# A two-layer decoder trunk in split fp32: the 512-column and the 256-column products of an output chunk, in two runs or turn about

## Chip, cores and metric

The kernel runs on one core of a Trainium2 chip, in one launch. The metric is the time of an execution on the device in microseconds (us); with one core, that core is the slowest. A profiled execution gives a span (first to last instruction) and a trace of every instruction.

## The reference, cut to what matters

A decoder trunk of two layers on 256 tokens of width 2048, all in fp32. Nearly all the work is products of a 256-row activation with a large weight matrix:

```python
def sq_relu_mlp(h, w1, w2):
    return jnp.square(jax.nn.relu(h @ w1)) @ w2          # w1 2048x8192, w2 8192x2048
...
    for l in range(DEPTH):                               # DEPTH = 2
        hn = rms_norm(x, mix_norm_g[l])
        x = x + (even_mixer(hn, ...) if l % 2 == 0 else odd_mixer(hn, ...))
        x = x + cross_attention(rms_norm(x, xattn_norm_g[l]), mem_n, xq_w[l], xk_w[l], xv_w[l], xo_w[l])
        x = x + sq_relu_mlp(rms_norm(x, mlp_norm_g[l]), mlp_w1[l], mlp_w2[l])
    return rms_norm(x, final_norm_g)
```

The even mixer is a convolution of 31 taps beside a differential attention, the odd mixer a gated convolution of 3 taps.

## The kernel before

**Split operands.** TensorE multiplies fp32r operands, which hold fewer bits than fp32, so each operand is split into a high part (the value rounded) and a low part (what is left). Weights come from memory as `raw` tiles (128x1024 f32, half of an output chunk's weights). ScalarE (ACT) casts `whi` from `raw`, and VectorE (DVE) subtracts to give `wlo`. An `Act` holds an activation with the high and the low part of each of its 16 blocks side by side, 256 columns each: `act.both(k)` is both (512 columns), `act.hi(k)` the high part alone (256 columns).

**An output chunk** is 128 output columns. It accumulates 16 blocks of 128 rows in one PSUM bank, and each block takes two products: high weights by both parts (512 columns wide), and low weights by the high part (256 columns). Two functions write them out:

- `long_run` (lines 217 to 225) has the whole chunk's four tiles `h[0], h[1], l[0], l[1]`. It issues fifteen 512-column products, then sixteen 256-column ones, then the last 512-column one, which closes the bank.
- `wide_piece` (lines 193 to 202) does the same with half a chunk, eight blocks: eight 512-column products (seven if this half closes the bank), eight 256-column ones, and the closing one.

By the code's loops 305 chunks go through `long_run` (the MLPs, most of the mixers' output projections and of the odd mixer) and 95 through `wide_piece` (the even mixer's projections, the keys of layer 0, the queries, and the first few chunks after a normalisation). That is 400 chunks, with 16 products of each width.

**What makes the tiles.** `weights` (line 178) loads, casts and subtracts for `wide_piece` and the mixers. In the MLPs an order written by hand does it: a `Chunk` (line 897) has `hi(g)` on ACT and `lo(g)` on DVE, or, where DVE is short of time, `lo_added(g)` (line 916): ACT writes the negated, rounded `raw` into `wlo`, and a DMA issued by GpSimd (POOL) adds `raw` to it in place (line 923). There are three `whi` and four `wlo` buffers, so tiles are made about one chunk ahead of their use.

**The MLP's order.** Its hidden layer comes in four quarters (`qd`). In each quarter 16 chunks of `w1` are followed by the `w2` part: eight times a `Step` (21 products of a fast 2x2 block scheme, tiles `sw`, `tw`, `b`, `hs`, PSUM tiles `p`), each followed by an output chunk of `w2` through `long_run`. The first of these, `outs[0]`, gets both its low halves by `lo_added`, first half 1 and then half 0 (lines 1213 and 1214), while the last chunk of `w1` runs:

```python
                if c == NC - 1 and seven:
                    n.lo_added(1)
                    n.lo_added(0)
```

This happens in each of four quarters of two MLPs, eight times in all.

**The even mixer's taps.** The 31 taps of eight channel blocks run on DVE (`cv`), dealt out a few per call of `weights` and put in one order with the `wlo` subtractions (the token "lo", line 190). They last until about 322 us, through the keys of layer 0.

TensorE (PE) issues in the order of the program. Outside the hand-ordered parts a scheduler places ACT's and DVE's instructions; it does so anew when the order on PE changes.

Of the kernel before, what the change touches and what calls it, by code (L numbers as in the profile page):

```python
# [45 lines left out]
def trunk(ctx: ExitStack, tc: tile.TileContext, d):  # L46
# [98 lines left out]
    def ordered(i, token):  # L145

        tc.stamp_issue_order_token(i.ins, token)
# [20 lines left out]
    def mm(*a, **k):  # L168
        i = T.matmul(*a, **k)  # L169
        if strict[0]:  # L170
            ordered(i, "pe")
# [21 lines left out]
    def wide_piece(ps, hi, lo, act, k, first, last):  # L193


        w = [slice(j * P, (j + 1) * P) for j in range(8)]
        for j in range(7 if last else 8):
            mm(ps, hi[:, w[j]], act.both(k + j), start=first and j == 0, stop=False)
        for j in range(8):
            mm(ps[:, :S], lo[:, w[j]], act.hi(k + j), start=False, stop=False)  # L200
        if last:
            mm(ps, hi[:, w[7]], act.both(k + 7), start=False, stop=True)

    def proj_group(srcs, act, order=(0, 1)):


        pp = [ps_mm.tile([P, 512], F32, tag="mm", name="mm") for _ in srcs]
        for g in order:
            if g == order[-1] and len(srcs) > 1:
                run_stages(END)  # L210
            for src, ps in zip(srcs, pp):
                hi, lo = weights(src[:, g * 1024:(g + 1) * 1024])
                first, last = g == order[0], g == order[-1]
                wide_piece(ps, hi, lo, act, g * 8, first, last)
        return pp

    def long_run(ps, h, l, act):

        w = [slice(j * P, (j + 1) * P) for j in range(8)]
        for k in range(15):  # L220
            mm(ps, h[k // 8][:, w[k % 8]], act.both(k), start=k == 0, stop=False)
        for k in range(16):
            mm(ps[:, :S], l[k // 8][:, w[k % 8]], act.hi(k), start=False, stop=False)
        mm(ps, h[1][:, w[7]], act.both(15), start=False, stop=True)
        return ps

    def proj_long(src, act):
        ps = ps_mm.tile([P, 512], F32, tag="mm", name="mm")
        h, l = zip(*[weights(src[:, g * 1024:(g + 1) * 1024]) for g in range(2)])
        return long_run(ps, h, l, act)  # L230
# [666 lines left out]
    class Chunk:  # L897
# [27 lines left out]
        def run(self, act, pool, tag):  # L925
            self.ps = long_run(pool.tile([P, 512], F32, tag=tag, name="mm"), self.h, self.l, act)
# [513 lines left out]
```

## Time and profile before

| | us |
|---|---|
| median of 3 runs | 2852.05 (2851.72 to 2854.14) |
| profiled execution | 2851.39 |
| its span | 2849.3 |
| PE busy | 2834.7 (99%) |
| PE weight loads busy | 2476.8 (87%) |
| DVE busy | 2318.8 (81%) |
| ACT busy | 1687.4 (59%) |
| POOL busy | 78.6 (3%) |

The profiled execution is 0.66 us under the median, and 2.1 us of it lie outside the span. An engine is busy while an instruction is open on it. Matmuls overlap their successors, so the distance from one start to the next, not the duration, is what a product costs. In rows of the timeline the columns are: start, time to the last end, engine, line, operation, what is written and read, sizes and count. Line 169 is the helper that issues every product, line 59 the one for ACT and DVE, so the rows are told apart by their tiles.

### The profile page before, as it was taken

The page shows a single profiled execution, that of the slowest core. Times are in us where ns is not written, and L with a number is a line of the kernel's source. Part 1 is how long each engine was busy: PE and PEld are TensorE (multiplying, and loading weights), DVE is VectorE, ACT ScalarE, POOL GpSimd, SP SyncE. Part 2 cuts the span into 40 slices and gives each one's busy share as a digit, 9 for nine tenths or more (in the row PEclk, how much of TensorE's full clock was granted, in tenths as well). Part 3 has the DMA queues.
Part 4 walks back from the last instruction along what each step waited for, and adds up shares of the span by engine and source line. Part 5 has one row for each costly group of instructions (what it writes and reads, how often), then busy time and mean ns, then how long its engine had stood idle before and what let it go on. Part 6 is the DMA issues. An engine that isn't in the chain of part 4 may idle for free.

```text
span 2849.3 us, 42240 instructions
## 1 busy us (share of the span) xinstructions
PE 2834.7 (99%) x15827; PEld 2476.8 (87%) x15827; DVE 2318.8 (81%) x3609; ACT 1687.4 (59%) x2365; POOL 78.6 (3%) x107
## 2 busy tenths in 40 slices
PE   9999999999999999999999999999999999999998
PEld 7888888898888888888888888888988888888887
DVE  7899987776788888888987787888777888888888
ACT  6666445555565665656654455676555656656566
POOL 0000000000000000000000000000000000000000
PEclk9999999999999999999999999999999999999999
DMA  7455665545686786967766666984455867769686
GB/s 247 162 183 176 191 193 187 172 151 177 194 255 197 223 241 200 265 193 236 214 201 199 197 208 222 255 259 151 149 177 192 258 207 220 233 201 265 193 243 170
DMA packets 213516, 588.23 MB, mean 206 GB/s; under 512 B 18240, under 2 KB 84160, under 8 KB 213312
## 3 DMA queue, kind: packets, MB, share of 16 engines
q1 hardware_dynamic: 200064, 538.48, 58.2%
q0 software_dynamic: 12672, 46.14, 8.2%
q8 instruction: 124, 2.03, 0.3%
q10 hardware_dynamic: 576, 0.92, 0.1%
q14 instruction: 80, 0.66, 0.1%
HBM read 537.23 MB, written 2.10 MB: 189 GB/s over the span
## 4 chain that ended last, share of the span: by engine, by line
PE 95%; DVE 2%; DMA 1%; ACT 1%; issue 0%; SPq 0%; DVEq 0%; ACTq 0%; POOLq 0%; POOL 0%
PE mm L169 75%; PE p L169 13%; PE mmr L169 4%; PE pox L169 1%; PE sx L169 1%; DVE wlo L59 1%; ACT whi L59 0%; DVE cv L59 0%; DMA wlo<-raw 0%; DVE x L59 0%; DMA raw<-w 0%; DMA raw<-even_in 0%; DMA raw<-odd_in 0%; DMA x<-xT 0%; PE nmr L169 0%
## 5 line engine op out<-in xcount | busy, mean ns | idle before, releaser
L59 ACT CAST whi<-raw 128x1024 fp32r<-128x1024 f32 (+1 forms) x849 | 890.3, 1050 | 398.5 <-PE mm L169 299.1
L59 DVE TENSOR_TENSOR wlo<-raw,whi 128x1024 fp32r<-128x1024 f32 (+1 forms) x761 | 924.1, 1220 | 94.3 <-ACT whi L59 84.2
L169 PE MATMUL mm<-xn,whi 128*128 128x512 f32 x3840 | 938.8, 392 | 0.0
L169 PEld LDWEIGHTS mm<-xn,whi 128*128 128x128 f32 x3840 | 701.7, 188 | 133.4 <-DVE xn L59 0.6
L169 PEld LDWEIGHTS mm<-xn,wlo 128*128 128x128 f32 x3840 | 501.0, 191 | 24.1 <-DVE wlo L59 0.2
L169 PE MATMUL mm<-xn,wlo 128*128 128x256 f32 x3840 | 509.0, 283 | 0.0
L59 ACT COPY sum<-mm 128x256 f32<-128x256 f32 x272 | 100.6, 371 | 382.9 <-PE mm L169 382.3
L169 PE MATMUL mm<-hid,whi 128*128 128x512 f32 x1024 | 253.3, 389 | 0.0
L59 ACT CAST tw<-raws 128x1024 fp32r<-128x1024 f32 x160 | 160.6, 1047 | 145.3 <-DVE raws L59 142.9
L59 DVE TENSOR_TENSOR raws<-raws 128x512 f32<-128x512 f32 x320 | 220.8, 690 | 7.7
L169 PEld LDWEIGHTS mm<-hid,whi 128*128 128x128 f32 x1024 | 192.5, 188 | 37.4
L59 DVE TENSOR_TENSOR sum<-mm,sum 128x256 f32<-128x256 f32 x240 | 101.0, 421 | 147.1 <-ACT sum L59 146.8
L59 DVE TENSOR_TENSOR tw<-raws,tw 128x1024 fp32r<-128x1024 f32 x160 | 189.6, 1222 | 26.5 <-ACT tw L59 24.9
L169 PE MATMUL p<-tw,hs 128*128 128x512 f32 x720 | 189.2, 389 | 0.0
L59 DVE TENSOR_TENSOR x<-x,mm 128x256 f32<-128x256 f32 x256 | 107.4, 420 | 80.9 <-PE mm L169 76.3
L169 PEld LDWEIGHTS p<-tw,hs 128*128 128x128 f32 x720 | 135.2, 188 | 28.0
L923 POOL DMA_DIRECT2D wlo<-raw x88 | 74.9, 855 | 2551.1 <-ACT wlo L59 1773.7
L169 PEld LDWEIGHTS mm<-hid,wlo 128*128 128x128 f32 x1024 | 131.1, 191 | 5.5 <-DMA wlo<-raw 0.7
L169 PE MATMUL mm<-hid,wlo 128*128 128x256 f32 x1024 | 132.9, 283 | 0.1
L169 PE MATMUL mm<-mem,whi 128*128 128x512 f32 x512 | 128.5, 392 | 0.0
L169 PE MATMUL mm<-o,whi 128*128 128x512 f32 x512 | 124.7, 392 | 0.0
L59 DVE TENSOR_TENSOR slo<-raws,shi 128x1024 fp32r<-128x1024 f32 x71 | 86.9, 1223 | 37.7 <-ACT shi L59 37.7
(224 smaller groups left out, 3235.4 us busy)
## 6 DMA issues: line engine op xcount, KB each, us to landing
raw<-w SPq DMA_DIRECT2D x384, 512.0 KB, 4.9
raws<-w SPq DMA_DIRECT2D x128, 512.0 KB, 5.3
raw<-odd_in SPq DMA_DIRECT2D x96, 512.0 KB, 4.8
wlo<-raw POOLq DMA_DIRECT2D x88, 512.0 KB, 7.4
raw<-even_in SPq DMA_DIRECT2D x64, 512.0 KB, 4.3
raw<-xk SPq DMA_DIRECT2D x64, 512.0 KB, 4.4
raw<-xq SPq DMA_DIRECT2D x64, 512.0 KB, 4.0
raw<-xo SPq DMA_DIRECT2D x64, 512.0 KB, 3.7
```

The source lines that it names most:

```text
L59: i = getattr(self.engine, name)(*a, **k)
L169: i = T.matmul(*a, **k)
L923: G.dma_start(out=self.l[g], in_=self.raw[g], accum_op=ALU.add)
```

## The change

In `wide_piece` and `long_run` the two runs become one loop over the blocks: the 512-column product of a block, then its 256-column product. The closing 512-column product of the bank stays last. The products, their operands and their number are the same.

```diff
@@ wide_piece
-        for j in range(7 if last else 8):
-            mm(ps, hi[:, w[j]], act.both(k + j), start=first and j == 0, stop=False)
         for j in range(8):
+            if not last or j < 7:
+                mm(ps, hi[:, w[j]], act.both(k + j), start=first and j == 0, stop=False)
             mm(ps[:, :S], lo[:, w[j]], act.hi(k + j), start=False, stop=False)
@@ long_run
-        for k in range(15):
-            mm(ps, h[k // 8][:, w[k % 8]], act.both(k), start=k == 0, stop=False)
         for k in range(16):
+            if k < 15:
+                mm(ps, h[k // 8][:, w[k % 8]], act.both(k), start=k == 0, stop=False)
             mm(ps[:, :S], l[k // 8][:, w[k % 8]], act.hi(k), start=False, stop=False)
```

On PE, at the head of the first `w2` chunk of a quarter (`outs[0]` of layer 0's first quarter), the order before is as follows; `p7` is the end of the step before it, `wlo_8551` is half 0 of the low weights and `wlo_8548` half 1, and `hid` are the quarters of the hidden activation.

```order
L169 MATMUL p7_8570<-tw_8283,hs_8010 128x512 x3
L169 MATMUL mm_8601<-hid_7952,whi_8544 128x512 x4
L169 MATMUL mm_8601<-hid_8172,whi_8544 128x512 x4
L169 MATMUL mm_8601<-hid_8390,whi_8599 128x512 x4
L169 MATMUL mm_8601<-hid_8571,whi_8599 128x512 x3
L169 MATMUL mm_8601<-hid_7952,wlo_8551 128x256 x4
L169 MATMUL mm_8601<-hid_8172,wlo_8551 128x256 x4
```

In the changed kernel the same place on PE reads:

```order
L169 MATMUL p7_8570<-tw_8283,hs_8010 128x512 x3
L169 MATMUL mm_8601<-hid_7952,whi_8544 128x512
L169 MATMUL mm_8601<-hid_7952,wlo_8551 128x256
L169 MATMUL mm_8601<-hid_7952,whi_8544 128x512
L169 MATMUL mm_8601<-hid_7952,wlo_8551 128x256
L169 MATMUL mm_8601<-hid_7952,whi_8544 128x512
```

The first use of `wlo_8551` moves from behind fifteen 512-column products to behind one.

On ACT, before and after, the rows that make these two tiles, in the same place behind the evacuation (`sum`) of the chunk before, are the same:

```order
L59 COPY sum_8542<-mm_8455 128x256
L59 CAST whi_8544<-raw_8488 128x1024
L59 ACTIVATE wlo_8548<-raw_8489 128x1024
L59 ACTIVATE wlo_8551<-raw_8488 128x1024
L59 ACTIVATE uu_8436<-sum_8542 128x256
```

So the making of the tile does not move on ACT, and POOL's order is the same as well.

On DVE, in the keys of layer 0 with the taps (`cv`) beside them, the two low halves of one chunk (`wlo_3274` and `wlo_3308`) stand before like this; `on` and `co` belong to the attention's output, `keys` evacuates the chunk before.

```order
L59 TENSOR_TENSOR on_3234<-orig_563,rb_3238 128x256
L59 SCALAR_TENSOR_TENSOR cv_571<-a_570,vec_95,cv_571 128x230
L59 TENSOR_TENSOR wlo_3274<-raw_3272,whi_3273 128x1024
L59 TENSOR_TENSOR co_3090<-on_3234,co_3090 128x256
L59 SCALAR_TENSOR_TENSOR cv_571<-a_570,vec_95,cv_571 128x229
L59 SCALAR_TENSOR_TENSOR cv_571<-a_570,vec_95,cv_571 128x228
L59 TENSOR_TENSOR keys_3013<-mm_3205,sum_3265 128x256
L59 SCALAR_TENSOR_TENSOR cv_571<-a_570,vec_95,cv_571 128x227
L59 TENSOR_TENSOR wlo_3308<-raw_3306,whi_3307 128x1024
```

In the changed kernel the scheduler gives:

```order
L59 SCALAR_TENSOR_TENSOR cv_571<-a_570,vec_95,cv_571 128x230
L59 TENSOR_TENSOR wlo_3274<-raw_3272,whi_3273 128x1024
L59 TENSOR_TENSOR on_3234<-orig_563,rb_3238 128x256
L59 SCALAR_TENSOR_TENSOR cv_571<-a_570,vec_95,cv_571 128x229
L59 SCALAR_TENSOR_TENSOR cv_571<-a_570,vec_95,cv_571 128x228
L59 TENSOR_TENSOR co_3090<-on_3234,co_3090 128x256
L59 TENSOR_TENSOR keys_3013<-mm_3205,sum_3265 128x256
L59 SCALAR_TENSOR_TENSOR cv_571<-a_570,vec_95,cv_571 128x227
L59 TENSOR_TENSOR wlo_3308<-raw_3306,whi_3307 128x1024
```

The first half moves ahead of one operation (`on`); ahead of the second half stand the same operations as before.

## The prediction

> **What bounds the kernel now.** I read the page first (busy shares, then the chain of work that ended last), then the timeline of PE, then the waits and landings of the tiles that PE reads.
>
> ```profile
> PE 2834.7 (99%) x15827; PEld 2476.8 (87%) x15827; DVE 2318.8 (81%) x3609; ACT 1687.4 (59%) x2365; POOL 78.6 (3%) x107
> PE 95%; DVE 2%; DMA 1%; ACT 1%; issue 0%; SPq 0%; DVEq 0%; ACTq 0%; POOLq 0%; POOL 0%
> L169 PE MATMUL mm<-xn,whi 128*128 128x512 f32 x3840 | 938.8, 392 | 0.0
> L169 PE MATMUL mm<-xn,wlo 128*128 128x256 f32 x3840 | 509.0, 283 | 0.0
> ```
>
> PE is busy 99% of the span and is 95% of the chain, and its products have no idle time before them. So two things can change the time: how far apart the same products start in another order, and holes that open on PE because an operand is now wanted earlier than it is there. What a product costs is read from starts. These are PE's rows in a steady stretch of the odd mixer, and the widths of single products around it:
>
> ```profile
> 1508.40 3.82 PE L169 MATMUL mm<-xn,whi 128*128 128x512 f32 x16
> 1512.06 2.08 PE L169 MATMUL mm<-xn,wlo 128*128 128x256 f32 x16
> 1513.97 3.82 PE L169 MATMUL mm<-xn,whi 128*128 128x512 f32 x16
> ...
> 1519.54 0.63 PE L169 MATMUL mm<-xn,whi 128*128 128x512 f32 x2
> ```
>
> ```profile
> L169 PE MATMUL mm<-xn,wlo x192: 277/283/283, 1500.9 to 1564.0; 128*128 128x256 f32 x192
> ```
>
> ```profile
> L169 PE MATMUL mm<-xn,whi x190: 389/389/398, 1499.8 to 1565.9; 128*128 128x512 f32 x190
> ```
>
> A chunk takes 5.57 us (1508.40 to 1519.54 is two). The 16 narrow products take 1513.97 - 1512.06 = 1.91 us, 119.4 ns each, or 120 without the first, which is 6 ns shorter (277 for 283).
>
> **The change, part by part.** Durations come from the one profiled execution: 2851.39 us, span 2849.3, 0.66 us under the median of the runs. No work is added or removed; PE's 6400 + 6400 products of this kind only change places. A measurement of this kernel can tell about 0.2% (5.7 us) from no change.
>
> *1. Eight waits for an accumulating DMA.* At the head of each quarter's `w2` part, `outs[0]` has its low halves made by ACT and a POOL DMA, half 1 first and half 0 second. This is layer 0's first quarter on PE, and the two DMAs with their time to landing:
>
> ```profile
> 817.78 0.40 PE L169 MATMUL mm<-xn,whi 128*128 128x512 f32 x1
> 818.02 1.54 PE L169 MATMUL p<-sw,hid 128*128 128x512 f32 x6
> ...
> 822.80 3.56 PE L169 MATMUL mm<-hid,whi 128*128 128x512 f32 x15
> 826.20 2.08 PE L169 MATMUL mm<-hid,wlo 128*128 128x256 f32 x16
> ```
>
> ```profile
> L923 POOL DMA_DIRECT2D wlo<-raw x2: 949/971/993, 815.3 to 816.2; - x2
> DMA to landing us min/median/max: 8.1/8.9/9.6
> ```
>
> Half 0 is issued at 816.2 and lands 9.6 us later, at 825.87. Before, PE first wants it at 826.20, after fifteen 512-column products of 3.40 us (226.7 ns each): these were its cover, with 0.33 us to spare. Now it is wanted after one of them, at 822.80 + 0.23 = 823.03, so PE stands for 2.84 us. PE issues in order, so the fourteen other 512-column products, ready since before, are queued behind the waiting one, and all later work of the chunk. ACT's order in front of the DMAs does not move, and its casts follow PE's end of the chunk before, so the DMA does not come earlier. Nothing takes the time back, since PE is the bound.
>
> The same happens in all eight quarters. Here is the one that lands last, and all 88 such DMAs with who waits for them:
>
> ```profile
> L923 POOL DMA_DIRECT2D wlo<-raw x2: 843/850/857, 2577.4 to 2578.4; - x2
> DMA to landing us min/median/max: 8.6/9.4/10.2
> ```
>
> ```profile
> 2584.95 3.56 PE L169 MATMUL mm<-hid,whi 128*128 128x512 f32 x15
> 2588.61 2.18 PE L169 MATMUL mm<-hid,wlo 128*128 128x256 f32 x16
> ```
>
> ```profile
> L923 POOL DMA_DIRECT2D wlo<-raw x88: 841/854/1150, 815.3 to 2824.8; - x88
> ...
>   PEld mm L169: 0.7, 2
> ...
> DMA to landing us min/median/max: 4.4/7.4/10.2
> ```
>
> Here PE started the narrow run late already (3.66 us after the wide one): two such waits, 0.7 us, stand in the trace of before. The second DMA of each pair is issued 6.2 to 6.6 us before its chunk starts and lands 8.9 to 10.2 us after that, so PE's wait is 2.2 to 3.4 us each. The eight sum to **22.5 us** (2.84, 2.24, 3.02, 2.91, 2.85, 2.45, 3.39, 2.79). Bounds: 8 x 2.1 = 17 if all land like the quickest, 8 x 3.4 = 27 like the slowest. The other 80 land before their chunk starts, or are a half 1, wanted only eight pairs (2.8 us) later.
>
> *2. The low halves of the even mixer's stage.* From 139 to 322 us DVE carries the taps and is nearly full:
>
> ```profile
> 139.00:232.00 93.00, 92.84 (x566) 81.26 (x565) 87.48 (x215) 62.19 (x122) 0.94 (x3) 1.00 0.55 181
> 232.00:322.00 90.00, 90.00 (x538) 79.37 (x537) 88.97 (x197) 48.58 (x82) 0.00 (x0) 1.00 0.54 175
> ```
>
> (PE, PE loads, DVE, ACT, POOL: DVE is busy 88.97 of the second 90 us.) A chunk of the keys, with its two low halves, and the latest low half of the stage:
>
> ```profile
> 275.51 2.23 PE L169 MATMUL mm<-mem,whi 128*128 128x512 f32 x9
> ...
> 278.66 0.71 PE L169 MATMUL mm<-mem,whi 128*128 128x512 f32 x2
> ```
>
> ```profile
> 274.92 1.22 DVE L59 TENSOR_TENSOR wlo<-raw,whi 128x1024 fp32r<-128x1024 f32 x1
> ...
> 277.95 1.22 DVE L59 TENSOR_TENSOR wlo<-raw,whi 128x1024 fp32r<-128x1024 f32 x1
> ```
>
> ```profile
> 199.07 1.78 PE L169 MATMUL mm<-xn,whi 128*128 128x512 f32 x7
> ```
>
> ```profile
> 199.33 1.22 DVE L59 TENSOR_TENSOR wlo<-raw,whi 128x1024 fp32r<-128x1024 f32 x1
> ```
>
> The first half ends at 276.14 and would be wanted at 275.74 + 0.23 = 275.97; the second ends at 279.17 and would be wanted at 278.89: 0.17 and 0.28 us late. The worst ends at 200.55 for 199.30, 1.25 us late. If DVE keeps its own pace, PE falls behind once, by the worst: 1.25 us. If DVE is held up as well (it evacuates PE's chunks, queued in the same order), each of the some 16 chunks of 5.8 us in the 90 us (two halves of 278.66 - 275.74 = 2.9) pays its 0.28 us again: 1.25 + 16 x 0.28 = 5.7 us. The new DVE order puts the first half ahead of one operation, not the second. I take **2.5 us**, nearer the lower end, as DVE's idle time is 1 us in 90. Elsewhere the tiles are ready before their chunk starts, mostly by over 1 us; a high tile is held up to 1 us longer, which its cover of a chunk's length takes.
>
> *3. The rate of the products themselves.* After a run of narrow products the next wide ones are slower: a chunk takes 5.57 us where 16 x (226.7 + 120) ns make 5.55, the settled rates of both runs. That is 0.02 us per turn, and there are 305 + 2 x 95 = 495 turns: 10 us, which go if an alternating pair costs what its halves cost in settled runs. Alternating pairs do not stand in the trace. Their ends: 389 with 277 ns in the rows above (6 under the settled 389 with 283), and 398 with 283 (9 over). A duration is the distance to the next start plus about 162 ns (389 for 226.7, 283 for 120), so that is -6 to +9 ns a pair, -38 to +58 us over 6400. The nearest rows are those of a lone wide product between narrow ones:
>
> ```profile
> L169 PE MATMUL mm<-xn,whi x1: 396/396/396, 559.5 to 559.5; 128*128 128x512 f32 x1
> ```
>
> ```profile
> L169 PE MATMUL pox<-pb,hl x1: 281/281/281, 559.8 to 559.8; 128*128 128x256 f32 x1
> ```
>
> It is 7 ns over, and the narrow one behind it 2 under: +5 a pair, 32 us. But the first narrow product after settled wide ones is 6 under and the first wide one after settled narrow ones 7 over, which about cancel: 0 a pair. I take the middle, +2.5 ns a pair, 16 us, less the 10 us of the turns: **+6 us**.
>
> By the formula of the Trainium skill (TensorE: Matmul & The Clock Gate, Back-to-back issue gap: columns over 2.4 GHz plus 2.5 ns) a product's cost does not depend on its neighbours, so part 3 would be nought, and the turns' 0.02 us would not be there; the trace's rows differ both from that and from its figures (216 and 109 ns, where 226.7 and 119.4 are measured).
>
> **Sum:** 22.5 + 2.5 + 6 = 31 us on 2851.4, with the median 0.7 above: 2883 us, 1.1% slower.
>
> **Rivals.**
>
> - *Faster: the pair settles low.* If each pair takes 389 with 277, part 3 is -38 - 10 = -48 us and the whole -48 + 25 = -23: 2829 us. It decides below -2.4 ns a pair (-15 us, with the turns' -10 against the 25 of the waits). For it: 277 stands behind every wide run. Against it: the one wide product alone between narrow ones is slow. Chance 0.10.
> - *The pair settles high,* at 398 with 283: +58 - 10 + 25 = +73, 2925 us. For it: two wide products behind narrow ones reach 398. Against: only the second does. Chance 0.10.
> - *The DMA waits do not come:* the DMAs land earlier, since their time to landing runs from 4.4 to 10.2 us. Then 2.5 + 6 = 8.5 us: 2861. Against it: all eight pairs were slow, since the second queues behind the first. Chance 0.06.
> - *The holes slow the clock.* In the trace PE's first eleven products take twice as long:
>
> ```profile
> 1.46 5.06 PE L108 MATMUL rest<-idle 128*128 128x512 f32 x11 [1.46 <-DVE zero L59]
> ```
>
> 4.86 us for 11, 442 ns each where 226.7 is settled: 2.4 us lost. Were each of the eight holes followed by such a stretch, 19 us come on top: 2902. The longest hole in the middle of the trace shows no such thing, but it is 1 us only (1.03 us behind the product at 1445.88):
>
> ```profile
> 1445.88 0.39 PE L169 MATMUL mm<-xn,whi 128*128 128x512 f32 x1
> 1447.14 0.40 PE L174 MATMUL nmb<-ident,rrow 128*128 128x128 f32 x2 [0.86 <-DVE rrow L59]
> ```
>
> Chance 0.05. The Trainium skill (the same page, Part 1: The HAM clock gate) has the clock halved after an idle window of about 3.4 us; by that, holes of 2.2 to 3.4 us are just too short.
>
> **How the numbers follow.** The forecast has the other 0.69. Its own ends: pair -1 ns with short waits, -6 - 10 + 17 + 1 = +2; pair +6 with long ones, 38 - 10 + 27 + 6 = +61. So the range is 2854 to 2913; it takes in the third and the fourth rival, and leaves out the first two. Faster by over 0.2% (under 2846) is the first rival: 0.10. Within 0.2% (2846 to 2858) are the lowest end of the forecast and part of the third rival: 0.09. Slower: 0.81.
>
> **What would show it.** In the profile after: PE's weight loads waiting for the DMA of `wlo` eight times, 2 to 3.5 us each, at the start of each quarter's first `w2` chunk; that shows part 1. Waits of PE for DVE's `wlo` between 139 and 322 us, a few us in all, show part 2. The distance between chunk starts in the steady stretch near 1510 us, 5.57 before, shows part 3: 5.59 by the forecast, 5.55 if pairs cost as settled runs do, 5.45 by the first rival, 5.69 by the second. The prediction is wrong if PE does not wait at `outs[0]`, or if the chunk distance leaves 5.53 to 5.65.

## The result, and the profile after

| | before | after |
|---|---|---|
| median of the runs, us | 2851.95 (2851.72 to 2854.14, 4 runs) | 2922.22 (2919.90 to 2923.54, 4 runs) |
| profiled execution: time, span, us | 2851.39, 2849.3 | 2922.5, 2920.6 |

The changed kernel is slower: ratio 1.0245, 95% interval 1.0233 to 1.0257. The forecast was 2883 with a range of 2854 to 2913; the measured median lies 9 us above that range. The direction was right; of the 70 us only 31 were foreseen.

The page of the changed kernel, first its busy shares, then the chain that ended last, then one group of products:

```profile
PE 2877.4 (99%) x15827; PEld 2480.8 (85%) x15827; DVE 2326.4 (80%) x3609; ACT 1690.7 (58%) x2365; POOL 78.6 (3%) x107
PE 90%; DMA 4%; DVE 4%; issue 1%; ACT 1%; SPq 0%; POOLq 0%; POOL 0%; DVEq 0%; ACTq 0%
...
L169 PE MATMUL mm<-hid,wlo 128*128 128x256 f32 x1024 | 284.1, 288 | 26.5 <-DMA wlo<-raw 26.5
```

PE is still busy 99%, on the same 15827 products, yet its busy time went from 2834.7 to 2877.4 us. So 43 of the 71 us of span were lost while PE counts as busy: the same products are further apart. The rest is idle time, and the last row gives the place and releaser of most of it: the low halves of `w2`, waiting for the accumulating DMA. The waits of PE and of its weight loads (engine, product, releaser: us, count, longest) have it in one line each:

```profile
PE mm L169 <- DMA wlo<-raw: 26.5, 8, 3.8
PE nmb L174 <- DVE rrow L59: 3.8, 2, 2.5
...
PE mm L169 <- DVE wlo L59: 0.4, 2, 0.3
```

```profile
PEld mm L169 <- DMA wlo<-raw: 29.9, 8, 4.2
PEld mm L169 <- DVE wlo L59: 3.1, 8, 0.6
```

Eight waits, one for each quarter of the two layers, as forecast. The first of them in PE's timeline (start, length of the row, engine, line, tiles; the wait in brackets):

```profile
830.52 0.39 PE L169 MATMUL mm<-hid,whi 128*128 128x512 f32 x1
834.61 0.58 PE L169 MATMUL mm<-hid,wlo 128*128 128x256 f32 x1 [3.70 <-DMA wlo<-raw]
834.99 0.63 PE L169 MATMUL mm<-hid,whi 128*128 128x512 f32 x1
835.42 0.41 PE L169 MATMUL mm<-hid,wlo 128*128 128x256 f32 x1
835.63 0.63 PE L169 MATMUL mm<-hid,whi 128*128 128x512 f32 x1
...
838.33 0.40 PE L169 MATMUL mm<-hid,whi 128*128 128x512 f32 x1
838.58 0.28 PE L169 MATMUL mm<-hid,wlo 128*128 128x256 f32 x1
838.70 0.40 PE L169 MATMUL mm<-hid,whi 128*128 128x512 f32 x1
```

Two things are to be seen. The narrow product could have started at 830.52 + 0.23 = 830.75 and starts at 834.61: a hole of 3.86 us. And the pairs behind the hole are 0.64 us apart (834.99 to 835.63) where those from 838.33 on are 0.37 apart. The windows of the same stretch (busy time and count on PE, PE loads, DVE, ACT, POOL; then the granted clock) say why:

```profile
826.00:830.50 4.50, 4.50 (x21) 3.74 (x20) 2.57 (x5) 3.51 (x5) 0.00 (x0) 1.00 1.09 272
830.50:834.00 3.50, 0.41 (x2) 0.00 (x0) 2.84 (x5) 1.36 (x3) 0.84 (x1) 1.00 0.96 192
834.00:838.00 4.00, 3.39 (x12) 2.97 (x13) 2.72 (x4) 1.38 (x2) 0.00 (x0) 0.57 0.94 246
838.00:842.00 4.00, 4.00 (x25) 3.45 (x24) 0.28 (x1) 1.28 (x2) 0.00 (x0) 1.00 0.99 347
```

The granted clock is 0.57 on average in the 4 us behind the hole and 1.00 on either side: PE runs at half clock for about 3.4 us, then at full clock again. Six of the eight holes have such a stretch behind them, of 3.41 or 6.83 us.

Why this hole is longer than the forecast 2.84 us stands in the pair of DMAs that it waits for (POOL's issues, then us from issue to landing):

```profile
L923 POOL DMA_DIRECT2D wlo<-raw x2: 950/973/996, 822.9 to 823.9; - x2
DMA to landing us min/median/max: 8.9/9.8/10.7
```

Half 0 is issued at 823.9, 6.6 us ahead of the chunk as before, but lands 10.7 us later where it took 9.6: 834.6, which is when PE starts.

The third thing is the steady stretch of the odd mixer. In the timeline each chunk begins with a joined row of two wide products:

```profile
1559.91 0.63 PE L169 MATMUL mm<-xn,whi 128*128 128x512 f32 x2
...
1565.56 0.63 PE L169 MATMUL mm<-xn,whi 128*128 128x512 f32 x2
...
1571.21 0.63 PE L169 MATMUL mm<-xn,whi 128*128 128x512 f32 x2
```

```profile
L169 PE MATMUL mm<-xn,wlo x187: 277/281/285, 1500.0 to 1565.4; 128*128 128x256 f32 x187
```

```profile
L169 PE MATMUL mm<-xn,whi x188: 395/398/404, 1499.7 to 1565.8; 128*128 128x512 f32 x188
```

A chunk takes (1571.21 - 1559.91) / 2 = 5.65 us, where it took 5.57. The wide products have a median of 398 ns where it was 389, the narrow ones 281 where it was 283: +7 ns a pair.

**Where the 71.3 us of span went**, worked out from the starts of PE's rows in both traces against the settled 226.7 and 120 ns:

| | us |
|---|---|
| rate of the products: over settled +37.8 after, +7.9 before | 30 |
| eight holes at `outs[0]`: 3.86, 3.79, 3.00, 3.51, 2.75, 3.18, 3.93, 3.78 | 27.8 |
| half clock behind six of them: what 30.7 us of such stretches cost | 12.7 |
| lateness of DVE's low halves | 2 |

These make 72.5, which is 1.2 us more than the span grew; where that goes was not traced.

### The profile page after: what moved, and what is told of

It is laid out like the page before. It is cut to its first block, busy times and chain, and to the rows that moved or that the text cites. A ratio compares the mean times of both kernels' runs of the same rounds, so it can differ in the third digit from the quotient of the medians.

```text
span 2920.6 us, 42239 instructions
## 1 busy us (share of the span) xinstructions
PE 2877.4 (99%) x15827; PEld 2480.8 (85%) x15827; DVE 2326.4 (80%) x3609; ACT 1690.7 (58%) x2365; POOL 78.6 (3%) x107
## 4 chain that ended last, share of the span: by engine, by line
PE 90%; DMA 4%; DVE 4%; issue 1%; ACT 1%; SPq 0%; POOLq 0%; POOL 0%; DVEq 0%; ACTq 0%
PE mm L169 72%; PE p L169 12%; PE mmr L169 4%; DMA wlo<-raw 3%; DVE wlo L59 1%; DMA raw<-w 1%; DVE cv L59 1%; PE sx L169 1%; PE pox L169 1%; ACT whi L59 0%; DVE sum L59 0%; DVE scm L59 0%; DMA x<-xT 0%; PE xt L174 0%; PE nmr L169 0%
## 5 line engine op out<-in xcount | busy, mean ns | idle before, releaser
L169 PE MATMUL mm<-xn,whi 128*128 128x512 f32 x3840 | 1347.1, 399 | 0.0
L169 PE MATMUL mm<-xn,wlo 128*128 128x256 f32 x3840 | 1040.5, 281 | 0.5 <-DVE wlo L59 0.4
L169 PEld LDWEIGHTS mm<-xn,wlo 128*128 128x128 f32 x3840 | 725.3, 189 | 24.6 <-DVE wlo L59 2.5
L169 PE MATMUL mm<-hid,whi 128*128 128x512 f32 x1024 | 377.8, 407 | 0.0
L169 PE MATMUL mm<-hid,wlo 128*128 128x256 f32 x1024 | 284.1, 288 | 26.5 <-DMA wlo<-raw 26.5
L169 PEld LDWEIGHTS mm<-hid,wlo 128*128 128x128 f32 x1024 | 199.6, 195 | 35.3 <-DMA wlo<-raw 29.9
L169 PE MATMUL mm<-mem,whi 128*128 128x512 f32 x512 | 182.2, 400 | 0.0
L169 PE MATMUL mm<-o,whi 128*128 128x512 f32 x512 | 178.9, 399 | 0.0
L169 PE MATMUL mm<-mem,wlo 128*128 128x256 f32 x512 | 138.9, 282 | 0.1
```

## The experiments

The theory behind the runs: three effects add up, each by itself. Alternating pairs cost about 6 ns more than settled runs (30 us), the holes are the DMA waits (28 us), and the half clock is caused by the holes (13 us). The rivals: the pairs are slow only behind holes or because the weight tile changes at every product; the half clock comes from the alternating stream itself.

### All but the eight heads alternate

The changed kernel, with the eight `outs[0]` chunks in two runs as before:

```diff
-        for k in range(16):
-            if k < 15:
+        group = 16 if head else 1
+        for g in range(0, 16, group):
+            for k in range(g, min(g + group, 15)):
                 mm(ps, h[k // 8][:, w[k % 8]], act.both(k), start=k == 0, stop=False)
-            mm(ps[:, :S], l[k // 8][:, w[k % 8]], act.hi(k), start=False, stop=False)
+            for k in range(g, g + group):
+                mm(ps[:, :S], l[k // 8][:, w[k % 8]], act.hi(k), start=False, stop=False)
...
-                    w.run(hid, ps_nm, "nm")
+                    w.run(hid, ps_nm, "nm", k == 0)
```

> The changed kernel with the eight first w2 chunks (outs[0]) back in two runs; all other chunks alternate. Theory: the loss has three parts that add up, holes for the DMA at these eight places (about 28 us), a halved clock behind them (about 13 us), and 6 ns more for each alternating pair (about 30 us with the turns between runs taken off, and 2 us of waits for DVE). Then the first two go: 2884 us (2879 to 2889), no wait of PE for the DMA of wlo, clock 1.00, a chunk every 5.64 us near 1510 us. Rival, the pairs cost 2.5 ns as I had forecast and the rest of the loss comes from the holes: 2861 us.

Measured: 2885.68 us (2884.68 to 2886.77), ratio to before 1.0118, interval 1.0104 to 1.0132. The time came as the theory expected; that PE would no longer wait for the DMA did not quite. Its waits of PE and its wide products in the same stretch:

```profile
PE mm L169 <- DMA wlo<-raw: 2.8, 5, 0.8
```

```profile
L169 PE MATMUL mm<-xn,whi x188: 395/398/403, 1499.9 to 1566.0; 128*128 128x512 f32 x188
```

The wide products are as slow as in the changed kernel (398), at a clock of 0.999 over the span and with the eight long holes gone (the longest left is 0.93 us): of the 33.6 us over before, some 30 are the pairs. So the pairs do not need the holes. That 2.8 us of waits stay shows again that the DMA pair lands later than before: fifteen wide products no longer cover it every time.

### Only the eight heads alternate

The kernel before, with `group = 1 if head else 16` in the same place, and `wide_piece` untouched.

> The kernel before, in which only the eight first w2 chunks (outs[0]) alternate. Theory: the holes and the clock alone: 28 + 13 = 41 us, 2893 us (2886 to 2898), with clock dips behind most of the eight holes. Rival, the dips need the alternating stream and not the hole: 2880 us and clock 1.00.

Measured: 2880.05 us (2878.86 to 2881.22), ratio 1.0098, interval 1.0084 to 1.0112. That is 28 us where some 41 were expected, so the theory missed here. The number is the rival's, but not for the rival's reason: the holes are there, and the clock is not 1.00 behind all of them. The waits of PE, the pair of DMAs of the first quarter, and the windows around its hole:

```profile
PE mm L169 <- DMA wlo<-raw: 19.6, 8, 2.7
```

```profile
L925 POOL DMA_DIRECT2D wlo<-raw x2: 952/974/996, 816.4 to 817.4; - x2
DMA to landing us min/median/max: 7.5/8.3/9.1
```

```profile
823.00:827.00 4.00, 1.82 (x9) 1.22 (x8) 3.35 (x6) 1.86 (x4) 0.84 (x1) 1.00 0.83 165
827.00:831.50 4.50, 4.50 (x19) 3.86 (x18) 3.09 (x4) 2.78 (x3) 0.00 (x0) 0.62 1.02 299
```

The holes are 2.06 to 2.91 us long (20.9 us in all), close to what the prediction had worked out, since the DMA lands 9.1 us after its issue and not 10.7. Only three of the eight have a half-clock stretch behind them (0.62 above). So the stretches do not need the alternating stream in all chunks; and the effects are not independent: where all chunks alternate, the holes are 0.86 us longer each (27.8 against 20.9), and the clock falls more often.

Why some holes are followed by half clock and others not can be read from the clock records of the traces. Within a run, the half-clock stretches in the middle of the program start on one grid with steps of 3.413 us: in the changed kernel the first starts at 834.32, and the others 156, 426, 478, 530 and 583 steps later. Cut time at this grid and count the idle part of each step, from starts as for the holes. The step just before a stretch has 2.06, 2.31 or 2.35 us of idle PE in this run, 2.11 to 3.41 us in the changed kernel, and 2.40 us in the next experiment. In no run does a stretch start behind a step with 1.94 us or less. (The start and the end of the program, where PE is idle in many small pieces, are left out of this count.) In the changed kernel the hole of 3.79 us falls across a grid line, at 1011.81, and the clock stays at 1.00:

```profile
1008.40:1011.81 3.41, 1.63 (x8) 1.01 (x6) 2.79 (x5) 1.97 (x3) 0.85 (x1) 1.00 0.95 192
1011.81:1015.22 3.41, 1.56 (x9) 1.39 (x10) 2.94 (x4) 1.99 (x2) 0.00 (x0) 1.00 0.98 184
```

It leaves 1.94 us idle in the first step (3.41 - 1.63, and 0.16 in which the last product before it still counts as busy) and 1.85 in the second. So what counts in these runs is how much of one step is idle, and a hole of 2 to 4 us is followed by half clock or not by where it falls on the grid. No run moved a hole along the grid to try this by itself.

The traces also suggest why the pair of DMAs lands later in the changed kernel. The two loads of `raw` tiles ahead of each pair wait for buffers that DVE's subtractions free. They are issued 4.6 us before the pair in the kernel before and in this run, on average over the eight places, and 3.9 us before it where all chunks alternate; the pair takes 10.5, 10.2 and 11.2 us from first issue to last landing. The run with the heads alone in runs has 3.9 and 11.3 us, so the delay comes with the alternation of the other chunks. That the closer loads are its cause was not tried by itself.

### Half 0 ahead of half 1

In the changed kernel the two lines that issue the accumulating DMAs change places, so that the half wanted first is issued first:

```diff
-                    n.lo_added(1)
                     n.lo_added(0)
+                    n.lo_added(1)
```

> The changed kernel with the order of the two accumulating DMAs of outs[0] swapped: half 0, which is wanted first, is issued first. Theory: half 0 lands some 8.3 us after its issue, about 1 us after it is wanted, and half 1 lands 2 to 3 us later, about when it is wanted: two short waits of 1.3 us together in place of 3.5, no clock dips (holes of about 1 us): 2922 - 28 - 13 + 10 = 2891 us (2885 to 2898). Rival, a hole of any length costs a clock dip: 2903 us.

Measured: 2889.67 us (2888.99 to 2890.51), ratio 1.0132, interval 1.0118 to 1.0146. As expected. The first quarter's hole, and the one place where the clock still falls in the middle of the program:

```profile
830.09 0.39 PE L169 MATMUL mm<-hid,whi 128*128 128x512 f32 x1
831.07 0.39 PE L169 MATMUL mm<-hid,wlo 128*128 128x256 f32 x1 [0.59 <-DMA wlo<-raw]
...
1466.02 0.41 PE L174 MATMUL nmb<-ident,rrow 128*128 128x128 f32 x2 [2.33 <-DVE rrow L59]
```

The hole at the head shrinks from 3.86 to 0.75 us (831.07 less 830.09 + 0.23), and no half clock follows it: the narrow product behind it has its usual 0.39 us, not 0.58. Behind the 2.5 us in front of `nmb`, at 1467.0, stands a half-clock stretch of 3.4 us, although no `w2` chunk is near. 32 us are gained by two lines, which shows that the holes and their clock stretches are the order of landing, not the amount of work.

### Only the chunks of `wide_piece` alternate

The kernel before with the first hunk of the change alone (`wide_piece`, 1520 of the 6400 pairs), so that no `w2` chunk is touched. These are the even mixer's projections, the keys of layer 0, the queries and the first chunks after a normalisation.

> The kernel before, in which only wide_piece alternates (95 chunks), long_run stays in runs. Theory: 95 x 16 x 6 ns = 9 us for the pairs, less 190 turns x 0.02 us = 4 us, and 2 us for low halves that come late from DVE: +7 us, 2859 us (2856 to 2863). Rival, the waits for DVE repeat in every chunk of the stage with the taps: +11 us or more, 2863 to 2866 us.

Measured: 2857.22 us (2856.49 to 2860.45, 11 runs), ratio 1.0019, interval 1.0010 to 1.0029. As expected, near the lower end: +5.2 us. Its weight loads' waits in the stage that the tapped keys share with DVE:

```profile
PEld mm L169 <- DVE wlo L59: 2.9, 8, 0.5
```

The same eight short waits as in the changed kernel (3.1 us). So PE does not wait again in every chunk, and the upper bound of that term, 5.7 us, is out.

### Runs of two, and runs of four

The first experiment again, with `group` 2 and then 4 for all but the heads, in both functions: the products go in twos (wide, wide, narrow, narrow), then in fours.

> Two wide products, then two narrow ones, and so on, in all chunks but the eight outs[0], which stay in two runs; to be set against alternation by one with the same outs[0] (2886 us). Theory: what costs is that wide products do not settle: in the trace of before it takes five of them behind a narrow one until they start 227 ns apart, so twos cost about 6 ns a pair like ones: 2885 us (2878 to 2892). Rival, each turn from narrow to wide costs 6 ns by itself: half the turns, 8 x 6 - 21 = 27 ns a chunk, 2852 + 11 + 2 = 2865 us.

> Four wide, then four narrow, in all chunks but the eight outs[0]. Theory (five wide products to settle): the four cost 7 + 9 + 2 + 6 = 24 ns more and the first two narrow ones 8 less, 16 ns a turn, 4 turns a chunk instead of one of 21: 63 - 21 = 42 ns a chunk, 2852 + 17 + 2 = 2871 us (2866 to 2876). Rival, 6 ns a turn: 2855 us.

Measured: twos 2869.38 us (2864.82 to 2870.49), ratio 1.0054, interval 1.0037 to 1.0071; fours 2866.27 us (2865.46 to 2867.93), ratio 1.0047, interval 1.0032 to 1.0062. At two the theory missed and the rival came near; at four the rival missed and the theory's lower end held. The wide products of both in the same stretch:

```profile
L169 PE MATMUL mm<-xn,whi x189: 390/395/400, 1500.0 to 1565.8; 128*128 128x512 f32 x189
```

```profile
L169 PE MATMUL mm<-xn,whi x190: 387/396/400, 1499.7 to 1565.8; 128*128 128x512 f32 x190
```

From the starts over the whole trace, a pair costs over the settled 346.7 ns, on average: 6.0 ns alternating, 2.9 in twos, 3.2 in fours, 1.25 in the runs of 8 and 16 of the kernel before. So one turn costs 6, 6, 13 and 20 ns: neither a fixed price for each turn nor a fixed number of wide products until the rate settles fits all four. Longer runs are cheaper on the whole, and how the loss arises inside stays open.

### The holes filled

The changed kernel, with fourteen products by a tile of zeros (96 columns) put between the first wide and the first narrow product of each `outs[0]`. They add nothing to the sum; PE works instead of standing still.

```diff
                 mm(ps, h[k // 8][:, w[k % 8]], act.both(k), start=k == 0, stop=False)
+            if head and k == 0:
+                for _ in range(14):
+                    mm(ps[:96], nought, act.both(0), start=False, stop=False)
```

> The changed kernel, and in the eight outs[0], between the first wide and the first narrow product, 14 products of 512 columns by a tile of zeros (14 x 0.227 = 3.2 us) that fill the hole; they add nothing to the sum. Theory: the wait for the DMA stays as long, but PE is busy in it, so the clock stays at 1.00 behind all eight: 2922 - 13 = 2909 us (2904 to 2914). Rival, the clock dips come of the stream and not of the idle PE: 2922 us with dips.

Measured: 2909.86 us (2909.27 to 2911.84), ratio 1.0200, interval 1.0185 to 1.0216. As expected. The head of the first quarter, and the windows of the same place:

```profile
830.26 0.39 PE L170 MATMUL mm<-hid,whi 128*128 128x512 f32 x1
830.49 3.33 PE L170 MATMUL mm<-hid,nought 128*96 128x512 f32 x14
833.75 0.39 PE L170 MATMUL mm<-hid,wlo 128*128 128x256 f32 x1
```

```profile
829.00:833.00 4.00, 4.00 (x20) 2.98 (x19) 3.38 (x5) 1.99 (x3) 0.84 (x1) 1.00 0.98 196
833.00:837.00 4.00, 4.00 (x23) 3.17 (x22) 3.43 (x5) 2.50 (x3) 0.00 (x0) 1.00 1.01 259
```

The narrow product starts as late as it would (3.26 us behind the end of the wide one), but the clock stays at 1.00, here and behind the other seven. The kernel is 12.4 us quicker than the changed one (2922.22 - 2909.86) by doing more: the half clock behind the holes comes from PE standing still, and it costs 12 to 13 us. The rival, that the alternating stream by itself slows the clock, is out.

### All products 512 columns wide

To part the alternation of weight tiles from the mix of widths, the low products are made 512 columns wide too, so that they add what the reference does not have. Once in the first experiment's order (alternating), once in the order of before (runs):

```diff
-            mm(ps[:, :S], lo[:, w[j]], act.hi(k + j), start=False, stop=False)
+            mm(ps, lo[:, w[j]], act.both(k + j), start=False, stop=False)
```

> High and low weights alternate block by block, but the low-weight product takes both parts of the activation as well, so it is 512 columns wide too (this adds the product of the two low parts); the eight outs[0] stay in two runs. Theory: the alternation of widths is what costs; with one width every product starts 227 ns after the one before: 2852 - 10 + 6400 x 0.107 = 3525 us. Rival, the alternation between two weight tiles is what costs, 6 ns a pair or more: 3563 us and starts more than 227 ns apart.

> The kernel before, in two runs, with the low-weight product 512 columns wide as well (it adds the product of the two low parts); to be set against the alternating one of the same widths, 3522.6 us. Theory: with one width the order of high and low weights costs nothing: 3520 to 3526 us, and products 227 ns apart everywhere, at the chunk borders too. Rival, alternation of weight tiles has a price that the other run hid: under 3515 us.

Measured, one execution each: alternating 3522.61 us, in runs 3524.45 us. Both as the theory expected. The high and the low products of the alternating one:

```profile
L169 PE MATMUL mm<-xn,wlo x89: 389/389/390, 1526.0 to 1565.8; 128*128 128x512 f32 x89
```

```profile
L169 PE MATMUL mm<-xn,whi x89: 388/389/390, 1525.7 to 1565.6; 128*128 128x512 f32 x89
```

All products stand at the settled 389 ns. With one width the order costs nothing, not even at the turns: the 30 us are the price of neighbours of different width, not of changing the weight tile at each product. That is shown for 512-column products; 256-column products from two tiles turn about, with no wide ones between, were not run.

## Why the prediction was wrong

*What bounds the kernel* held: PE is the bound, and nothing took lost time back.

*Part 1, the eight waits* (22.5 us): the mechanism was right, in place, number and cause, which the swap of the two DMAs and the run with only the heads both show. The size was 5 us short (27.8). With only the heads alternating it is 20.9, so the working was sound for the trace that it was read from; the step "the DMA does not come earlier" was true but left out that it could come later, and the whole change delays its landing by 0.7 us on average over the eight and by up to 1.6 us.

*Part 2, DVE's low halves* (2.5 us): right, about 2 us, and the lower of the two bounds was the one to lean to, as it was.

*Part 3, the rate of the products* (+6 us): this step failed, and it is the largest part of the miss. "I take the middle, +2.5 ns a pair" stood between 0 and +5; the runs show 6.0 ns a pair over the settled rate, and 30 us in place of 6. The row that counted was the one nearest to the new order, the lone wide product between narrow ones (396 and 281 ns, +5 a pair, 32 us less the 10 of the turns). The wide product in it had exactly the new neighbours on both sides, and it was averaged with rows at the edge of long runs, which have them on one side only. Its bounds, -6 to +9 ns, did hold the value. The chunk distance came out at 5.65 us, on the edge that the prediction had set for being wrong.

*The turns* (10 us, taken as gone): the start rows give 7.9 us before, so this was about right.

*The rivals*: the fourth one, that the holes slow the clock, happened beside the forecast and not in its place: 12.7 us where 19 were worked out, because six holes of eight were followed by it. Two reasons had set its chance at 0.05. One was that a hole of 1 us in the middle of the trace had nothing behind it; but the trace of before has a longer one at its end, which was passed over:

```profile
2839.99 0.40 PE L174 MATMUL nmb<-ident,rrow 128*128 128x128 f32 x2 [2.46 <-DVE rrow L59]
```

```profile
2840.50:2849.00 8.50, 0.00 (x0) 0.00 (x0) 4.87 (x9) 0.00 (x0) 0.00 (x0) 0.50 0.65 248
```

PE stands for about 2.6 us in front of `nmb`, and from 2840.45 on the granted clock is 0.50. No product follows, so it costs nothing there, but it was a sign that holes of the forecast's length can halve the clock. The other reason was a rule. By the Trainium skill (TensorE: Matmul & The Clock Gate, Part 1: The HAM clock gate) the clock halves after an idle window of about 3.4 us, and the holes were taken as too short. The trace disagrees in the threshold: in the run with only the heads alternating the clock halves behind three holes that are all shorter than 3 us, and in another run behind one of 2.5 us. That half-clock stretches last 3.41 us or twice that agrees with the 3.4 us that the Trainium skill gives for its window.

The second rival, with 2925 us, comes within 3 us of the measured time, but by luck: it has 58 us for the pairs, where 38 over the settled rate were measured, and nothing for the clock. The first and the third did not happen: the pairs did not settle low, and all eight waits came.

*The range*: 24 (pairs) + 13 (clock) + 5 (longer holes) make 42, against the 39 by which the median exceeds the forecast. Any one of the three would have stayed inside 2913. The cases were treated as exclusive, and the three risks, all on the same side, add up in one kernel.

No version that beats the kernel before came out of the runs.

## What to carry to other kernels

Where the order of work is changed on the engine that sets the time, look for the row in the trace that already has the new neighbours, and take its price undiluted: 6 ns a pair are nothing to see and 30 us in sum. A run of ready products at the head of a chunk is cover for the operands that come behind them; before spreading them, compare the landing of the last operand with the time at which it is wanted now. And where a change opens idle time on PE, price the half-clock stretch that can follow each hole (about 2 us here) beside the hole itself, and add the risks up rather than choosing among them.

## What the runs showed of the hardware that was not expected

- **Products of 512 and of 256 columns slow each other.** Settled by themselves they start 226.7 and 120 ns apart. Alternating, the starts repeat over three pairs: 236, 232, 241 ns behind a wide product, 113, 118, 120 behind a narrow one, 353 ns a pair in place of 346.7 (6.6 ns more in that stretch, 6.0 on average over the trace). With one width of 512 columns, alternating the same weight tiles costs nothing (389 ns rows throughout).
- **Half clock behind holes of 2 to 4 us.** In the changed kernel six of eight holes (2.75 to 3.93 us) had a stretch at half clock behind them, but not those of 3.79 and 3.00 us; with only the heads alternating, three of eight (2.06 to 2.91 us). So length alone does not decide it: the stretches start on a grid of 3.413 us, behind steps with 2.06 us or more of idle PE, and none starts behind steps with 1.94 us or less (read from the clock records, the start and the end of the program left out). A stretch lasts one step, 3.41 us, where the hole reaches at most 0.29 us into it, and two, 6.83 us, where it reaches 0.74 to 1.82 us into it. It costs about 2 us on average (12.7 by six).
- **One and the same DMA pair lands up to 1.6 us later.** The second DMA of the same pair took 9.1 us with only the heads alternating, 9.6 in the kernel before and 10.7 in the changed one, all in the first quarter, with the same bytes and the same two issues about 1 us apart on POOL; the loads on SP's queue stood 0.7 us closer to it in the last. Whether these loads are the reason was not tried.
